# Small fp32 products of both chunks interleaved over the array, and index dots on 64 rows, in a two-layer hybrid decoder trunk

## Chip, cores and metric

The kernel runs on one core of a Trainium2 chip. The metric is the device time of one execution in microseconds (us), the median of several runs; lower is better.

## What is computed

Two decoder layers act on x of 256 tokens by 1024 features, all in float32. Each layer normalises x, makes one wide projection, feeds three token mixers (a gated DeltaNet, a pooling mixer, a sparse attention), gates and merges their outputs, and adds one output projection to x. Two places matter here.

The sparse attention picks for every query the 64 causal keys with the largest index score. There are 4 index heads of 64 features, and one index key per position that all heads share:

```
dots = einsum('bqhd,bsd->bqhs', qi, ki)             # 4 heads, 64 features
score = einsum('bqh,bqhs->bqs', wi, relu(dots))     # weighted sum over heads
score = where(causal, score, -inf);  _, idx = top_k(score, 64)
```

The DeltaNet works by chunks and needs for every chunk and head the inverse of a unit lower triangular matrix:

```
lmat = where(strict, einsum('id,jd->ij', k_beta, k) * decay, 0)
tmat = triangular_solve(eye + lmat, eye)
u = tmat @ v_beta;  w = tmat @ (k_beta * exp(gc))
```

The kernel uses two chunks of 128 tokens (the reference's chunk of 64 is a matter of association, not of result), so there are 2 chunks x 4 heads = 8 matrices of 128 x 128 a layer.

## The kernel before

**Work and staging.** Weights come from HBM in 512 KB pieces (tile raw, SyncE's queue). Each is split into an upper part wh (a cast, on ScalarE or VectorE) and a remainder wl (a subtraction on VectorE), so that a product of float32 numbers becomes three fast matmuls (wslot, lines 679 to 690). These full matmuls, 128 rows by 128 columns of the array with 256 or 512 columns streamed, write the PSUM banks called pj and are most of TensorE's work. All smaller products write the four banks called mx. Small ones are plain fp32 and leave two matmul records each in the trace.

**Index dots** (lines 865 to 903). Queries of 128 tokens are transposed into qiT[t]: two heads side by side, the first head's 64 features on rows 0 to 63, the second's on rows 64 to 127. The shared key is transposed into two tiles kiT[0] and kiT[1] (128 rows, 256 columns), zeroed at the start: kiT[0] holds the key on rows 0 to 63 and zeros below, kiT[1] the other way round (lines 670 to 672, 871 and 872). So a dot of one head is a product over all 128 rows, half of them zeros. For each of the two query blocks (t = 0 sees 128 keys, t = 1 sees 256) and each pair of heads, two dots go to one bank, ScalarE applies the ReLU, and VectorE sums with the weights wiw into score. Eight rounds of max and match_replace find the top 64.

**The triangular inverse** (lines 1154 to 1229). First VectorE inverts the four 32 x 32 diagonal blocks of all 8 matrices together in xi, 31 steps of shuffle, multiply and add (the 32-wide solve). Then the off-diagonal parts follow on TensorE in four stages, each a set of small products, a copy out of PSUM, and the next:

- p1: per chunk and head, for a = 0 and 1 (rows 0 to 31 and rows 64 to 95), 32 x 32 products, written to rows 32 to 63 and 96 to 127; copied to y1
- p2: 32 x 32 products from y1 and xi on rows 32 to 63 and 96 to 127; copied into q4 and, transposed, into tt
- p3: per chunk and head one 64 x 64 product from rows 0 to 63, written to rows 64 to 127; copied to y2
- p4: per chunk and head one 64 x 64 product from rows 64 to 127, written to rows 0 to 63; copied into q4, the finished inverse Qm[c]

The source rows of a product set which rows of the array it uses, the rows it is written to which columns. In every stage all heads of chunk 0 come first, then those of chunk 1, and both chunks use the same places.

**What sets the order.** The program only lists operations; a planner (class Plan, lines 185 to 543) simulates five engine queues and writes out an order for all of them. Each operation has a price (cost, line 221), a priority in program order for TensorE and a due time for the others; six passes are made and the one with the least planned time is kept. Copies listed for ScalarE and elementwise work listed for POOL may go to VectorE where the planner finds that better. On TensorE a change between small and full products is priced at SWITCH = 103 ns, and for REST = 2500 ns after a return to full products, full ones go first. What counts as small is the filled share of the array, rows times columns over 16384 (fill, below 0.3 before). All instructions are issued from one line (543), so the profile names that line for everything; groups are told apart by tiles and shapes.

Of the kernel before, what the change touches and what calls it, by code (L numbers as in the profile page):

```python
# [15 lines left out]
T = 256  # L16
# [168 lines left out]
class Plan:  # L185
# [35 lines left out]
    def cost(self, eng, call, args, kw):  # L221


        out = args[0]
        n = int(np.prod(out.shape[1:])) if len(out.shape) > 1 else 1
        if call == "dma_start":
            run = int(args[1].shape[-1]) * 4
            rate = 120.0 if run < 512 else 262.0 if run < 1024 else 318.0 if run < 4096 else 338.0
            return 550.0 if eng == "POOL" else 475.0, n * out.shape[0] * 4 / rate, False
        if eng == "PE":  # L230
            if call == "transpose":
                return 109.0, 170.0, False
            if args[1].ap.dtype == F32R:
                return (n / 2.4 + 13.3 if n > 100 else 60.0), 175.0, False
            m, k = args[1].shape[-1], args[1].shape[0]
            if k <= 32:
                return 21.0, 170.0, False
            if k <= 64:
                return 134.0, 170.0, False
            return 2 * (max(n, m) / 1.2 + 3), 170.0, False  # L240
        srcs = [a for a in args[1:] if isinstance(a, Ref)]
        space = [r.tile.tag.psum for r in srcs]
        ps = any(space)
        w = max([int(np.prod(r.shape[1:])) for r in srcs] + [n])
        acc = kw.get("accum_out") is not None
        if eng == "ACT":
            hold = (18 if ps else 78) + 0.875 * w
            if isinstance(kw.get("bias"), Ref) or isinstance(kw.get("scale"), Ref):
                hold += 100
            return hold + (120 if acc else 0), (95 if ps else 22) + (90 if acc else 0), False  # L250
        if eng == "POOL":
            if kw.get("op") == ALU.pow:
                return 405.0 + 151 * n, 10.0, False
            if call == "memset":
                return 50 + 0.8 * n, 50.0, False
            return 90 + 2.2 * w, 60.0, True
        if call == "reciprocal":
            return 70 + 6.0 * w, 80.0, False
        fast = call in ("tensor_copy", "tensor_scalar") and not ps and not out.tile.tag.psum
        hold = 66 + (0.52 if fast or call == "memset" else 1.045) * w  # L260
        if call in ("scalar_tensor_tensor", "tensor_scalar") and any(isinstance(a, Ref) for a in args[2:3]):
            hold += 58
        if call == "stream_shuffle":
            hold += 40
        if call == "transpose":
            hold = 464.0
        two = [r for r in ([args[1], args[2]] if call == "tensor_tensor" else
                           [args[1], args[3]] if call == "scalar_tensor_tensor" else [])]
        port = fast or (bool(two) and not any(isinstance(r, Ref) and r.tile.tag.psum for r in two))
        return hold + (65 if acc else 0), 80.0 + (30 if acc else 0), port  # L270
# [81 lines left out]
    def lay_out(self):  # L352
# [63 lines left out]
        def pick(e):  # L416

            while soon[e] and not live(soon[e][0]):
                heapq.heappop(soon[e])
            while now[e] and not live(now[e][0]):  # L420
                heapq.heappop(now[e])
            t = free[e]
            while soon[e] and soon[e][0][0] <= t:
                q = heapq.heappop(soon[e])
                if live(q):
                    heapq.heappush(now[e], q[1:])
            if not now[e]:
                while soon[e] and not live(soon[e][0]):
                    heapq.heappop(soon[e])
                if not soon[e]:  # L430
                    return None
                q = soon[e][0][1:]
                return clear(self.ops[q[1]], e, soon[e][0][0]), e, q
            if e == "PE" and not small and t < whole + REST and fill(self.ops[now[e][0][1]]) < 0.3:
                for q in heapq.nsmallest(40, now[e]):
                    if live(q) and fill(self.ops[q[1]]) > 0.9:
                        return t, e, q
            first = now[e][0]
            at = clear(self.ops[first[1]], e, t)
            if at > t:  # L440
                for q in heapq.nsmallest(12, now[e]):
                    o = self.ops[q[1]]
                    if live(q) and clear(o, e, t) <= t and held(o, e) <= at - t + SLACK:
                        return t, e, q
            return at, e, first
# [5 lines left out]
        while len(order) < len(self.ops):  # L451
# [47 lines left out]
                        z.reader, z.until = e, at + o.cost + o.tail + 36.0  # L499
            o.start = at  # L500
            if e == "PE":
                part = fill(o) < 0.3
                free[e] = clock.run(at, o.cost + (SWITCH if part != small else 0.0), fill(o))
                if small and not part:
                    whole = at
# [42 lines left out]
def trunk(ctx: ExitStack, tc: tile.TileContext, x, norm_g, w_in, gate_b, conv_w, a_log, dt_bias, dn_onorm,  # L548
# [118 lines left out]
    plan.shift = 0  # L667
    ipad = make("ipad", [128, 384])
    G.memset(ipad, 0.0)
    kiT = [make(f"kiT{i}", [128, T], F32) for i in range(2)]  # L670
    for i in range(2):
        G.memset(kiT[i], 0.0)


    def rsqrt(dst, src):
        G.tensor_tensor(dst, src, mhalf[:, :src.shape[-1]], op=ALU.pow)
# [31 lines left out]
    for l in range(DEPTH):  # L708
# [141 lines left out]
        for t in range(2):  # L850
# [18 lines left out]
            S.copy(qt, pq[:, :256])  # L869
            qiT.append(qt)  # L870
            for i in range(2):
                S.copy(kiT[i][64 * i:64 * i + 64, t * 128:(t + 1) * 128], pq[0:64, 256:384])

        wiw = make("wiw", [128, 2, 4], F32)
        V.tensor_scalar(wiw, sm[:, :, 0:4], 1.0 / 16, None, op0=ALU.mult)
# [3 lines left out]
        for t in range(2):  # L879
            n = 128 * (t + 1)  # L880
            acc = make("score", [128, 256], F32)
            for pr in range(2):
                pd = bank("mx")
                for i in range(2):
                    mm(pd[:, i * 256:i * 256 + n], qiT[t][:, pr * 128:(pr + 1) * 128], kiT[i][:, :n], True, True)
                rl = unit()
                S.activation(v2(rl)[:, :, :n], v2(pd)[:, :, :n], AF.Relu)
                for i in range(2):
                    h = pr * 2 + i
                    w = wiw[:, t, h:h + 1]  # L890
                    if h == 0:
                        V.tensor_scalar(acc[:, :n], v2(rl)[:, i, :n], w, None, op0=ALU.mult)
                    else:
                        V.scalar_tensor_tensor(acc[:, :n], v2(rl)[:, i, :n], w, acc[:, :n], op0=ALU.mult, op1=ALU.add)
            V.tensor_tensor(acc[:, n - 128:n], acc[:, n - 128:n], con("ncaus"), op=ALU.add)
            top = small(8, "top")
            for r in range(8):
# [295 lines left out]
        y1 = unit().rearrange("p (a n j) -> p a n j", a=2, n=8)  # L1193
        pairs = [(a, slice(64 * a, 64 * a + 32), slice(64 * a + 32, 64 * a + 64)) for a in range(2)]

        for c in range(2):
            c4 = slice(4 * c, 4 * c + 4)
            p1 = bank("mx")[:, :256].rearrange("p (a h j) -> p a h j", a=2, h=4)
            for h in range(4):
                for a, lo32, hi32 in pairs:  # L1200
                    mm(p1[hi32, a, h], v4(Um[c])[lo32, h, hi32], tt[lo32, 4 * c + h, 0:32], True, True)
            for a, lo32, hi32 in pairs:
                (S.copy if a else V.tensor_copy)(y1[hi32, a, c4], p1[hi32, a])
        Qm = []
        for c in range(2):
            c4 = slice(4 * c, 4 * c + 4)
            u4 = v4(Um[c])
            q = unit()
            q4 = v4(q)
            G.tensor_tensor(q.rearrange("p (h b j) -> p h b j", h=4, b=4),  # L1210
                            xi[:, c4, None, :].to_broadcast([128, 4, 4, 32]),
                            con("bd").rearrange("p (b j) -> p b j", b=4)[:, None, :, :]
                            .to_broadcast([128, 4, 4, 32]), op=ALU.mult)
            p2 = bank("mx")[:, :256].rearrange("p (a h j) -> p a h j", a=2, h=4)
            for h in range(4):
                for a, lo32, hi32 in pairs:
                    mm(p2[lo32, a, h], y1[hi32, a, 4 * c + h], xi[hi32, 4 * c + h], True, True)
            V.transpose(tt[32:64, c4, 0:32], p2[0:32, 0])
            for a, lo32, hi32 in pairs:
                S.copy(q4[lo32, :, hi32], p2[lo32, a])  # L1220
            p3 = bank("mx").rearrange("p (a h j) -> p a h j", a=2, h=4)
            for h in range(4):
                mm(p3[64:128, 0, h], u4[0:64, h, 64:128], tt[0:64, 4 * c + h], True, True)
            y2 = unit()[:, :256].rearrange("p (h j) -> p h j", h=4)
            V.tensor_copy(y2[64:128], p3[64:128, 0])
            for h in range(4):
                mm(p3[0:64, 1, h], y2[64:128, h], q4[64:128, h, 64:128], True, True)
            S.copy(q4[0:64, :, 64:128], p3[0:64, 1])
            Qm.append(q)


        yah = make("y", [128, 4, T], F32R)
# [154 lines left out]
```

## Time and profile before

| | us |
|---|---|
| median of 3 runs | 568.51 (568.05 to 568.52) |
| the profiled execution | 569.16 |
| its span, first to last instruction | 567.1 |
| TensorE busy | 560.5 |
| VectorE busy | 507.3 |
| ScalarE busy | 301.0 |
| POOL busy | 30.8 |

The engines are PE (TensorE matmuls), PEld (TensorE weight loads), DVE (VectorE), ACT (ScalarE), POOL and SP (SyncE, which issues the transfers). A group of instructions is named by what it writes and reads, as in mx<-kiT,qiT; the tile name u stands for many general work tiles. A row of the timeline gives the start, the time from the first start to the last end of a merged group, the engine, the operation with the tiles, the active rows*columns of the array, the operand's shape, and the count; in brackets stands idle time before it and what ended that. Matmuls are pipelined: a record's length is far longer than the step from one start to the next, and the step is what a matmul costs.

### The profile page before, as it was taken

The page shows a single profiled execution, that of the slowest core. Times are in us where ns is not written, and L with a number is a line of the kernel's source. Part 1 is how long each engine was busy: PE and PEld are TensorE (multiplying, and loading weights), DVE is VectorE, ACT ScalarE, POOL GpSimd, SP SyncE. Part 2 cuts the span into 40 slices and gives each one's busy share as a digit, 9 for nine tenths or more (in the row PEclk, how much of TensorE's full clock was granted, in tenths as well). Part 3 has the DMA queues.
Part 4 walks back from the last instruction along what each step waited for, and adds up shares of the span by engine and source line. Part 5 has one row for each costly group of instructions (what it writes and reads, how often), then busy time and mean ns, then how long its engine had stood idle before and what let it go on. Part 6 is the DMA issues. An engine that isn't in the chain of part 4 may idle for free. (4 is left out here: it accounts for less than half of the span.)

```text
span 567.1 us, 9577 instructions
## 1 busy us (share of the span) xinstructions
PE 560.5 (99%) x3462; PEld 495.0 (87%) x3462; DVE 507.3 (89%) x1140; ACT 301.0 (53%) x575; POOL 30.8 (5%) x45
## 2 busy tenths in 40 slices
PE   8999999999999999999999999999999999999997
PEld 7888999999888887888879889999998888888886
DVE  4999999999999999688599999999999999968672
ACT  6756556564553435554366644756484444345520
POOL 4300100001000000010010002000100000000000
PEclk9999999999999999999999999999999999999999
DMA  8884865472776666444546459457466767454512
GB/s 295 205 278 111 231 156 145 127 223 96 241 236 202 207 202 189 166 129 153 180 132 192 125 143 252 113 150 205 115 189 208 210 202 218 127 181 141 174 39 74
DMA packets 89791, 98.68 MB, mean 174 GB/s; under 512 B 5616, under 2 KB 58656, under 8 KB 89744
## 3 DMA queue, kind: packets, MB, share of 16 engines
q1 hardware_dynamic: 89184, 97.47, 58.1%
q0 software_dynamic: 560, 0.60, 0.6%
q8 instruction: 27, 0.44, 0.3%
q14 instruction: 20, 0.16, 0.1%
HBM read 97.01 MB, written 1.05 MB: 173 GB/s over the span
## 5 line engine op out<-in xcount | busy, mean ns | idle before, releaser
L543 ACT CAST wh<-raw 128x1024 fp32r<-128x1024 f32 (+1 forms) x168 | 175.6, 1050 | 137.9 <-PE pj L543 107.4
L543 DVE TENSOR_TENSOR wl<-raw,wh 128x1024 fp32r<-128x1024 f32 (+1 forms) x174 | 209.3, 1212 | 10.6 <-issue 2.9
L543 PE MATMUL pj<-wh,hl 128*128 128x512 f32 (+1 forms) x352 | 101.5, 388 | 0.5 <-DVE hl L543 0.5
L543 PE MATMUL pj<-wl,hh 128*128 128x512 f32 (+1 forms) x352 | 101.4, 388 | 0.0
L543 PE MATMUL pj<-wh,hh 128*128 128x512 f32 (+1 forms) x352 | 100.6, 387 | 0.5 <-ACT hh L543 0.5
L543 PEld LDWEIGHTS pj<-wh,hl 128*128 128x128 f32 x352 | 64.9, 188 | 13.9 <-DVE hl L543 2.0
L543 PEld LDWEIGHTS pj<-wh,hh 128*128 128x128 f32 x352 | 64.7, 188 | 12.8 <-ACT hh L543 1.1
L543 PEld LDWEIGHTS pj<-wl,hh 128*128 128x128 f32 x352 | 64.8, 188 | 11.8
L543 PE MATMUL pj<-hh,wl 128*128 128x256 f32 x384 | 55.3, 284 | 0.0
L543 PE MATMUL pj<-hh,wh 128*128 128x256 f32 x384 | 55.1, 285 | 0.0
L543 PE MATMUL pj<-hl,wh 128*128 128x256 f32 x384 | 54.4, 283 | 0.0
L543 PE MATMUL pj<-wh,y 128*128 128x512 f32 (+1 forms) x208 | 50.5, 381 | 0.0
L543 PEld LDWEIGHTS pj<-hh,wh 128*128 128x128 f32 x384 | 49.8, 192 | 0.2
L543 PEld LDWEIGHTS pj<-hh,wl 128*128 128x128 f32 x384 | 50.0, 192 | 0.0
L543 PEld LDWEIGHTS pj<-hl,wh 128*128 128x128 f32 x384 | 49.6, 192 | 0.0
L543 PEld LDWEIGHTS pj<-wh,y 128*128 128x128 f32 x208 | 38.7, 188 | 7.6
L543 PE MATMUL mx<-wh,y 128*128 128x512 f32 (+1 forms) x128 | 38.4, 380 | 0.0
L543 PEld LDWEIGHTS mx<-u,u 128*128 128x128 f32 (+2 forms) x336 | 30.9, 165 | 3.8 <-issue 1.8
L543 PE MATMUL mx<-u,u 128*128 128x128 f32 (+2 forms) x336 | 32.5, 249 | 0.6 <-DVE u L543 0.5
L543 DVE SCALAR_TENSOR_TENSOR u<-pj,pt,u 128x255 f32<-128x255 f32 (+2 forms) x72 | 29.6, 474 | 0.2 <-ACT u L543 0.2
L543 PE MATMUL pj<-wl,y 128*128 128x512 f32 (+1 forms) x104 | 28.4, 382 | 0.0
L543 PEld LDWEIGHTS mx<-wh,y 128*128 128x128 f32 x128 | 23.3, 188 | 4.4 <-DVE y L543 0.2
(204 smaller groups left out, 677.4 us busy)
## 6 DMA issues: line engine op xcount, KB each, us to landing
raw<-in_w_in_dram SPq DMA_DIRECT2D x128, 512.0 KB, 4.2
raw<-in_w_branch_dram SPq DMA_DIRECT2D x24, 512.0 KB, 3.8
raw<-in_w_out_dram SPq DMA_DIRECT2D x16, 512.0 KB, 3.5
tg<-in_gate_b_dram SPq DMA_DIRECT2D x12, 256.0 KB, 4.3
raw<-in_w_in_dram SPq DMA_DIRECT2D x4, 486.0 KB, 5.4
x_sb<-in_x_dram SPq DMA_DIRECT2D x2, 512.0 KB, 4.5
out_dram<-x_sb SPq DMA_DIRECT2D x3, 256.0 KB, 2.0
raw<-in_w_in_dram SPq DMA_DIRECT2D x2, 324.0 KB, 4.2
```

What stands on the lines that cost most here:

```text
L543: getattr(self.real[o.eng], o.call)(*[put(a) for a in o.args], **{k: put(v) for k, v in o.kw.items()})
```

## The change

- The two zero-padded key tiles become one tile with the key on rows 0 to 63 and again on rows 64 to 127; the memsets go.
- A dot takes only the 64 rows of its head. Heads on rows 0 to 63 and heads on rows 64 to 127 alternate; heads of one half share a bank, so that each ReLU covers heads h and h + 2.
- In p1 to p4 the head loop is outside and the chunk loop inside, so products of chunk 0 and chunk 1 alternate, and chunk 1 is written to other rows (in p1 and p2 the 32 rows beside those of chunk 0, in p3 and p4 the other half), that is, uses other columns of the array. Each stage is done for both chunks before the next is listed.
- The planner's prices for small products change, and its bound for a small product rises from 0.3 to 0.6 of the array, which takes in the dots (64 x 128, 0.5).

```diff
--- before.py
+++ after.py
@@ -234,9 +234,9 @@
                 return (n / 2.4 + 13.3 if n > 100 else 60.0), 175.0, False
             m, k = args[1].shape[-1], args[1].shape[0]
             if k <= 32:
-                return 21.0, 170.0, False
+                return 16.0, 170.0, False
             if k <= 64:
-                return 134.0, 170.0, False
+                return 58.0 * max(n / 64.0, 1.0), 170.0, False
             return 2 * (max(n, m) / 1.2 + 3), 170.0, False
         srcs = [a for a in args[1:] if isinstance(a, Ref)]
         space = [r.tile.tag.psum for r in srcs]
@@ -431,7 +431,7 @@
                     return None
                 q = soon[e][0][1:]
                 return clear(self.ops[q[1]], e, soon[e][0][0]), e, q
-            if e == "PE" and not small and t < whole + REST and fill(self.ops[now[e][0][1]]) < 0.3:
+            if e == "PE" and not small and t < whole + REST and fill(self.ops[now[e][0][1]]) < 0.6:
                 for q in heapq.nsmallest(40, now[e]):
                     if live(q) and fill(self.ops[q[1]]) > 0.9:
                         return t, e, q
@@ -499,7 +499,7 @@
                         z.reader, z.until = e, at + o.cost + o.tail + 36.0
             o.start = at
             if e == "PE":
-                part = fill(o) < 0.3
+                part = fill(o) < 0.6
                 free[e] = clock.run(at, o.cost + (SWITCH if part != small else 0.0), fill(o))
                 if small and not part:
                     whole = at
@@ -667,10 +667,7 @@
     plan.shift = 0
     ipad = make("ipad", [128, 384])
     G.memset(ipad, 0.0)
-    kiT = [make(f"kiT{i}", [128, T], F32) for i in range(2)]
-    for i in range(2):
-        G.memset(kiT[i], 0.0)
-
+    kiT = make("kiT", [128, T], F32)
 
     def rsqrt(dst, src):
         G.tensor_tensor(dst, src, mhalf[:, :src.shape[-1]], op=ALU.pow)
@@ -869,7 +866,7 @@
             S.copy(qt, pq[:, :256])
             qiT.append(qt)
             for i in range(2):
-                S.copy(kiT[i][64 * i:64 * i + 64, t * 128:(t + 1) * 128], pq[0:64, 256:384])
+                S.copy(kiT[64 * i:64 * i + 64, t * 128:(t + 1) * 128], pq[0:64, 256:384])
 
         wiw = make("wiw", [128, 2, 4], F32)
         V.tensor_scalar(wiw, sm[:, :, 0:4], 1.0 / 16, None, op0=ALU.mult)
@@ -879,19 +876,21 @@
         for t in range(2):
             n = 128 * (t + 1)
             acc = make("score", [128, 256], F32)
+
+            pd = [bank("mx") for _ in range(2)]
             for pr in range(2):
-                pd = bank("mx")
                 for i in range(2):
-                    mm(pd[:, i * 256:i * 256 + n], qiT[t][:, pr * 128:(pr + 1) * 128], kiT[i][:, :n], True, True)
-                rl = unit()
-                S.activation(v2(rl)[:, :, :n], v2(pd)[:, :, :n], AF.Relu)
-                for i in range(2):
-                    h = pr * 2 + i
-                    w = wiw[:, t, h:h + 1]
-                    if h == 0:
-                        V.tensor_scalar(acc[:, :n], v2(rl)[:, i, :n], w, None, op0=ALU.mult)
-                    else:
-                        V.scalar_tensor_tensor(acc[:, :n], v2(rl)[:, i, :n], w, acc[:, :n], op0=ALU.mult, op1=ALU.add)
+                    mm(v2(pd[i])[:, pr, :n], qiT[t][64 * i:64 * i + 64, pr * 128:(pr + 1) * 128],
+                       kiT[64 * i:64 * i + 64, :n], True, True)
+            rl = [unit() for _ in range(2)]
+            for i in range(2):
+                S.activation(v2(rl[i])[:, :, :n], v2(pd[i])[:, :, :n], AF.Relu)
+            for h in range(4):
+                w, r = wiw[:, t, h:h + 1], v2(rl[h % 2])[:, h // 2, :n]
+                if h == 0:
+                    V.tensor_scalar(acc[:, :n], r, w, None, op0=ALU.mult)
+                else:
+                    V.scalar_tensor_tensor(acc[:, :n], r, w, acc[:, :n], op0=ALU.mult, op1=ALU.add)
             V.tensor_tensor(acc[:, n - 128:n], acc[:, n - 128:n], con("ncaus"), op=ALU.add)
             top = small(8, "top")
             for r in range(8):
@@ -1193,40 +1192,44 @@
         y1 = unit().rearrange("p (a n j) -> p a n j", a=2, n=8)
         pairs = [(a, slice(64 * a, 64 * a + 32), slice(64 * a + 32, 64 * a + 64)) for a in range(2)]
 
+
+        c4s = [slice(4 * c, 4 * c + 4) for c in range(2)]
+        b1, b2 = ([bank("mx")[:, :256].rearrange("p (a h j) -> p a h j", a=2, h=4) for _ in range(2)]
+                  for _ in range(2))
+        for h in range(4):
+            for c in range(2):
+                for a, lo32, hi32 in pairs:
+                    mm(b1[c][(hi32, lo32)[c], a, h], v4(Um[c])[lo32, h, hi32], tt[lo32, 4 * c + h, 0:32], True, True)
         for c in range(2):
-            c4 = slice(4 * c, 4 * c + 4)
-            p1 = bank("mx")[:, :256].rearrange("p (a h j) -> p a h j", a=2, h=4)
-            for h in range(4):
-                for a, lo32, hi32 in pairs:
-                    mm(p1[hi32, a, h], v4(Um[c])[lo32, h, hi32], tt[lo32, 4 * c + h, 0:32], True, True)
             for a, lo32, hi32 in pairs:
-                (S.copy if a else V.tensor_copy)(y1[hi32, a, c4], p1[hi32, a])
-        Qm = []
+                (S.copy if a else V.tensor_copy)(y1[hi32, a, c4s[c]], b1[c][(hi32, lo32)[c], a])
+        Qm = [unit() for _ in range(2)]
         for c in range(2):
-            c4 = slice(4 * c, 4 * c + 4)
-            u4 = v4(Um[c])
-            q = unit()
-            q4 = v4(q)
-            G.tensor_tensor(q.rearrange("p (h b j) -> p h b j", h=4, b=4),
-                            xi[:, c4, None, :].to_broadcast([128, 4, 4, 32]),
+            G.tensor_tensor(Qm[c].rearrange("p (h b j) -> p h b j", h=4, b=4),
+                            xi[:, c4s[c], None, :].to_broadcast([128, 4, 4, 32]),
                             con("bd").rearrange("p (b j) -> p b j", b=4)[:, None, :, :]
                             .to_broadcast([128, 4, 4, 32]), op=ALU.mult)
-            p2 = bank("mx")[:, :256].rearrange("p (a h j) -> p a h j", a=2, h=4)
-            for h in range(4):
+        for h in range(4):
+            for c in range(2):
                 for a, lo32, hi32 in pairs:
-                    mm(p2[lo32, a, h], y1[hi32, a, 4 * c + h], xi[hi32, 4 * c + h], True, True)
-            V.transpose(tt[32:64, c4, 0:32], p2[0:32, 0])
+                    mm(b2[c][(lo32, hi32)[c], a, h], y1[hi32, a, 4 * c + h], xi[hi32, 4 * c + h], True, True)
+        for c in range(2):
+            V.transpose(tt[32:64, c4s[c], 0:32], b2[c][(pairs[0][1], pairs[0][2])[c], 0])
             for a, lo32, hi32 in pairs:
-                S.copy(q4[lo32, :, hi32], p2[lo32, a])
-            p3 = bank("mx").rearrange("p (a h j) -> p a h j", a=2, h=4)
-            for h in range(4):
-                mm(p3[64:128, 0, h], u4[0:64, h, 64:128], tt[0:64, 4 * c + h], True, True)
-            y2 = unit()[:, :256].rearrange("p (h j) -> p h j", h=4)
-            V.tensor_copy(y2[64:128], p3[64:128, 0])
-            for h in range(4):
-                mm(p3[0:64, 1, h], y2[64:128, h], q4[64:128, h, 64:128], True, True)
-            S.copy(q4[0:64, :, 64:128], p3[0:64, 1])
-            Qm.append(q)
+                S.copy(v4(Qm[c])[lo32, :, hi32], b2[c][(lo32, hi32)[c], a])
+        half = slice(0, 64), slice(64, 128)
+        b3 = [bank("mx").rearrange("p (a h j) -> p a h j", a=2, h=4) for _ in range(2)]
+        for h in range(4):
+            for c in range(2):
+                mm(b3[c][half[1 - c], 0, h], v4(Um[c])[0:64, h, 64:128], tt[0:64, 4 * c + h], True, True)
+        y2 = [unit()[:, :256].rearrange("p (h j) -> p h j", h=4) for _ in range(2)]
+        for c in range(2):
+            (S.copy if c else V.tensor_copy)(y2[c][64:128], b3[c][half[1 - c], 0])
+        for h in range(4):
+            for c in range(2):
+                mm(b3[c][half[c], 1, h], y2[c][64:128, h], v4(Qm[c])[64:128, h, 64:128], True, True)
+        for c in range(2):
+            S.copy(v4(Qm[c])[0:64, :, 64:128], b3[c][half[c], 1])
 
 
         yah = make("y", [128, 4, T], F32R)
```

## Rows read from the trace of the kernel before

**Rows 1.** The page, busy time of each engine, and the granted clock in 40 slices.
```profile
PE 560.5 (99%) x3462; PEld 495.0 (87%) x3462; DVE 507.3 (89%) x1140; ACT 301.0 (53%) x575; POOL 30.8 (5%) x45
...
PEclk9999999999999999999999999999999999999999
```

**Rows 2.** Waits of TensorE, longest and last line; first and last long piece of the chain.
```profile
PE mx L543 <- POOL wh L543: 1.1, 1, 1.1
...
PE pj L543 <- DVE hl L543: 0.5, 1, 0.5
...
363.10 1.56 PE mx L543 x14
...
562.50 1.45 PE pj L543 x12
```

**Rows 3.** Stretches: us, busy PE, PEld, DVE, ACT, POOL, clock, DMA share, GB/s.
```profile
60.00:90.00 30.00, 29.67 (x251) 29.49 (x250) 30.00 (x70) 17.35 (x33) 2.02 (x2) 1.00 0.77 203
...
150.00:180.00 30.00, 30.00 (x134) 24.85 (x133) 28.85 (x93) 13.85 (x16) 0.00 (x0) 1.00 0.68 205
...
210.00:240.00 30.00, 29.48 (x229) 24.37 (x229) 23.76 (x47) 15.04 (x29) 1.29 (x1) 1.00 0.56 183
...
480.00:510.00 30.00, 30.00 (x235) 25.04 (x234) 24.32 (x48) 12.55 (x25) 0.94 (x1) 1.00 0.53 163
```

**Rows 4.** Timeline of TensorE where the first 32-row products start, both layers.
```profile
221.15 0.69 PE L543 MATMUL mx<-u,u 32*32 32x32 f32 x32 [0.52 <-DVE u L543]
...
489.99 0.69 PE L543 MATMUL mx<-u,u 32*32 32x32 f32 x32
```

**Rows 5.** Matmuls by shape: count | busy us, mean ns of one | idle before.
```profile
L543 PE MATMUL mx<-u,u 64*64 64x64 f32 x64 | 4.6, 221 | 0.0
...
L543 PE MATMUL mx<-kiT,qiT 128*128 128x256 f32 x16 | 3.8, 379 | 0.0
...
L543 PE MATMUL mx<-kiT,qiT 128*128 128x128 f32 x16 | 2.1, 277 | 0.0
...
L543 PE MATMUL mx<-xi,u 32*32 32x32 f32 x64 | 1.4, 192 | 0.0
```

**Rows 6.** Timeline around the index dots of layer 0.
```profile
34.51 1.10 PE L543 MATMUL mx<-kiT,qiT 128*128 128x128 f32 x8
...
37.16 1.89 PE L543 MATMUL mx<-kiT,qiT 128*128 128x256 f32 x8
...
39.34 0.63 PE L543 MATMUL pj<-wh,hh 128*128 128x512 f32 x2
...
39.60 0.28 DVE L543 TENSOR_SCALAR score<-u,wiw 128x128 f32<-128x128 f32 x1
```

**Rows 7.** Timeline of TensorE around a run of 32-row products, layer 0.
```profile
223.75 0.86 PE L543 MATMUL pj<-wh,hl 128*128 128x512 f32 x3
...
224.54 0.69 PE L543 MATMUL mx<-xi,u 32*32 32x32 f32 x32
...
225.16 0.51 PE L543 MATMUL pj<-wh,hl 128*128 128x512 f32 x1
...
225.51 1.08 PE L543 MATMUL pj<-wl,hh 128*128 128x512 f32 x4
```

**Rows 8.** Timeline around a run of 64-row products, layer 0.
```profile
227.88 1.00 PEld L543 LDWEIGHTS mx<-u,u 64*64 64x64 f32 x16 [0.35 <-issue]
227.88 1.14 PE L543 MATMUL mx<-u,u 64*64 64x64 f32 x16
...
229.52 1.09 PE L543 MATMUL pj<-wl,hh 128*128 128x512 f32 x4
...
229.76 1.05 ACT L543 CAST wh<-raw 128x1024 fp32r<-128x1024 f32 x1 [1.71 <-issue]
...
230.45 1.07 PE L543 MATMUL pj<-wh,hh 128*128 128x512 f32 x4
```

**Rows 9.** Timeline of TensorE, 227.80 to 228.00 us: records running there.
```profile
227.88 0.32 PE L543 MATMUL mx<-u,u 64*64 64x64 f32 x2
```


## The prediction

> **What bounds the kernel now.** I read the page first. TensorE's row says 99% of the span, VectorE's 89%, and the granted clock is at full in every slice [rows 1]. A busy share of 99% can hide waits, since matmuls are pipelined, so the waits and the chain come next. TensorE has five lines of waits, from 1.1 us in all (at the start) down to 0.5 each, and the chain of waits is TensorE work without a break from 363.10 us to its last piece at 562.50 [rows 2]. So TensorE is the bound: time taken off it is time off the span, as long as the others keep up. The table by stretch shows where that is doubtful. VectorE is as good as full from 30 to 210 us (six stretches, 28.85 to 30.00 of each 30), and has over 5 us of air in each 30 where the small products run (210 to 240 and 480 to 510) [rows 3]. What VectorE does in the full stretch ends in the 32-wide solve. Just then, at 221.15, TensorE waits 0.52 us for it; in the second layer, at 489.99, it doesn't [rows 4].
>
> All instructions share one helper line, so I go by shapes. An fp32 product leaves two matmul records. The index dots are 16 records of 128 columns and 16 of 256, the 32-row products 64 records in p1 and 64 more in p2, the 64-row products 64 [rows 5]. The whole change lies in these.
>
> **The change, part by part.**
>
> *Index dots, their pace.* Today every dot takes all 128 rows, half of them zeros. In layer 0 the short run is 8 records over 1.10 us, the last 0.275 long: (1.10 - 0.275)/7 = 0.118 us a record, 0.94 for 8. The long run is (1.89 - 0.38)/7 = 0.216 a record, 1.73 for 8 [rows 5, 6]. Both layers: 5.3 us. On 64 rows a record streams as many columns, so I count it the same when alone; the gain is that the heads on rows 0 to 63 and 64 to 127 may run side by side. No row shows 64-row, 128-column products doing so. Bounds: pace unchanged (0), or two at a time (-2.65 us). The nearest row is the run of 32-row products, which today alternates rows 0 to 31 with 64 to 95: 32 records, (0.69 - 0.19)/31 = 0.016 us a step [rows 7]. The 64-row run stays on one place of the array and steps by (1.14 - 0.22)/15 = 0.061 [rows 8]. Half the columns alone would make 0.031; the alternation gives 0.016. So two row groups do overlap, and I take -2.65.
>
> *Index dots, the way in and out.* A small product between full ones costs extra. Between 223.75 and 225.51 lie four full matmuls and one 32-row run: 1.76 us, less 4 x 0.23 (full ones step by 0.93/4, four of them from 229.52 to 230.45), less 32 x 0.016 = 0.51, leaves 0.33 [rows 7, 8]. Full-row dots pay none of it on leaving today: the last of the long run starts at 37.16 + 1.51 = 38.67 and streams for 0.216, to 38.89; two full matmuls later, 0.45, the next starts, at 39.34 [rows 6]. Half-row dots will pay, if using part of the array is what costs: 4 runs x 0.33 = +1.3 (bounds 0 and 1.3; I take 1.3, from the only small run whose surroundings I sum). The dots net -1.3 us, -0.65 a layer.
>
> *64-row products.* Four runs of 16 records at 0.061 are 3.9 us [rows 5, 8]. Now chunk 0 and chunk 1 alternate on the two column halves, over the same 64 rows. Bounds: 0, or half, -1.95. Only the 32-row run shows neighbours overlapping, and they differ in rows and columns at once, so nothing isolates columns; it is still the nearest, and I take half. In the 64-row run the weight loads (16 in 1.00 us) lie beside the matmuls (16 in 1.14, the same start) on the same rows [rows 8]. The Trainium skill, "TensorE: Matmul & The Clock Gate", Part 3, The mechanism, says that a weight load overlaps a running matmul only where the row group differs. By that rule this term would be 0 and the sum -1.65; the trace disagrees as far as one place of the array goes.
>
> *32-row products.* Four runs of 32 records, 0.51 each, 2.05 us [rows 5, 7]. They alternate two row groups already; the second chunk now comes between, on other columns. Bounds 0 and -1.0; by the same step I take -1.0. Their entering and leaving stays, 8 times.
>
> *What costs nothing.* Copies, transposes and VectorE's score sums keep number and shape. The copy of y2 for chunk 1 now prefers ScalarE, which sits idle for 1.71 us there [rows 8]. A ReLU now waits for all four dots, not two; VectorE first sums scores at 39.60, over 4 us after the first run of dots ended and 0.7 after the second [rows 6]. Without that cover the scores would come up to one run of dots, under 1 us, later into a full VectorE. The two memsets that fall away are the idlest engine's, POOL's (5% busy), at the start [rows 1]; it has nothing urgent behind them. No DMA is added or moved.
>
> *The order.* The kernel's planner gets new prices for these products and treats dots as small ones, so every queue is laid out anew and a dot can be held back up to 2.5 us behind full matmuls. Nothing in the trace prices that; I bound it by the waits it already has [rows 2]: one of 0.5 us gone, or as much again as its five lines hold, some 3 us. One part I can place: the 0.65 us that the first layer's dots save lies ahead of the full VectorE stretch, and at 221.15 TensorE already waits for VectorE [rows 3, 4]. I count it as lost there.
>
> *Sum.* -1.3 - 1.95 - 1.0 + 0.65 = -3.6 us. The profiled execution took 569.16 us (span 567.1 and 2.1 around it): it would come to 565.6. It stands 0.65 above the median of 568.51, against which the sum gives **564.9 us**.
>
> **Rivals.**
>
> *Columns alone bring nothing.* If products on the same rows take turns whatever their columns, the last two gains go: -0.65 to -1.3, 567.2 to 567.9 us. For it: no row shows two column places at once. Against: the 32-row step of 0.016, which two row groups share without a hint of a common limit.
>
> *The new order gives it back.* TensorE arrives earlier at the solve, and between the four small stages it needs full matmuls whose weights VectorE has split. If the wait at 221.15 grows by what was saved upstream, one like it opens at 489.99 and a half-microsecond opens before each of two or three stages, 2 to 3 us return: 567 to 568.5. For it: VectorE full. Against: its air where the small products stand, and a second layer with no wait there.
>
> *Slower: weight loads come out from behind the matmuls.* With each record on another place than the last, over rows in use, the load could have to wait for the matmul before. The first step of a run, where no matmul hides the load, shows that price: two 64-row records cover 0.32 us, the second 0.22 long, so 0.10 instead of 0.061 [rows 9]. At 0.04 on 64 records that is +2.6; with the dots' 0.65 and no gain on the 32-row runs it makes 568.5 + 1.9 = 570.4 us. It ends slower once the 64-row step exceeds 0.061 + (0.65 + 1.14)/64 = 0.089. The Trainium skill's rule above, taken strictly, would do this. Against: the loads lie beside matmuls on one place today.
>
> **How the numbers follow.** A measurement tells about 0.2%, 1.14 us, from no change: faster is below 567.4, slower above 569.6. The forecast has 0.52; its own range, from full gain with a lucky order to 2 us of loss, is 562.6 to 566.5. Columns bring nothing: 0.20, half faster, half same. The order gives it back: 0.16, split 0.06 faster, 0.08 same, 0.02 slower. Loads exposed: 0.12, slower. So 0.68 faster, 0.18 same, 0.14 slower. The range, 562.6 to 569.3, takes in the second and nearly all of the third case, and leaves out the last.
>
> **What would show it.** Right: dots in runs with a mean step near 0.108 (256 columns) and 0.058 (128); 64-row runs of 16 records within 0.7 us instead of 1.14, 32-row runs within 0.45 instead of 0.69; about 0.3 us of entering and leaving around each run of dots; TensorE still 99% busy and the chain on it to the end. Wrong: a 64-row step at or above 0.06, a dot step still at 0.216, or waits of TensorE for VectorE that sum to over 3 us more.

## The result, and the profile after

| | before | changed |
|---|---|---|
| median, 6 runs each, us | 568.34 (568.05 to 568.76) | 563.87 (563.61 to 564.15) |
| profiled execution, us | 569.16 | 563.87 |
| its span, us | 567.1 | 561.8 |

The ratio is 0.9919, 95% interval 0.9909 to 0.9929: 4.5 us or 0.8% faster. The forecast was 3.6 us less.

The page of the changed kernel, to be held against [rows 1]:

```profile
span 561.8 us, 9576 instructions
...
PE 555.9 (99%) x3462; PEld 489.3 (87%) x3462; DVE 508.2 (90%) x1142; ACT 300.3 (53%) x574; POOL 28.3 (5%) x42
```

TensorE is still the bound, at 99%, with the same number of matmul records; VectorE and ScalarE are as busy as before to 1 us. So as much is done as before, and TensorE is done with it sooner. Its waits, against [rows 2]:

```profile
PE mx L543 <- POOL wh L543: 1.1, 1, 1.1
PE mx L543 <- DVE big L543: 0.7, 2, 0.5
PE pj L543 <- DVE hl L543: 0.5, 1, 0.5
PE pj L543 <- ACT hh L543: 0.4, 1, 0.4
```

The line for VectorE's u, the 0.5 us ahead of the first 32-row products in layer 0, is gone. The timeline of TensorE shows that place and the runs of the first layer's inverse, against [rows 4, 7, 8]:

```profile
220.42 0.61 PE L543 MATMUL pj<-wh,hh 128*128 128x512 f32 x2
220.97 0.45 PE L543 MATMUL mx<-u,u 32*32 32x32 f32 x32
...
223.75 0.39 PE L543 MATMUL pj<-wh,hh 128*128 128x512 f32 x1
224.07 0.45 PE L543 MATMUL mx<-xi,u 32*32 32x32 f32 x32
224.45 0.96 PE L543 MATMUL pj<-wh,hh 128*128 128x512 f32 x3
225.25 1.08 PE L543 MATMUL pj<-wh,hl 128*128 128x512 f32 x4
226.17 1.07 PE L543 MATMUL pj<-wl,hh 128*128 128x512 f32 x4
227.17 0.68 PE L543 MATMUL mx<-u,u 64*64 64x64 f32 x16
227.78 1.19 PE L543 MATMUL pj<-wh,hh 128*128 128x512 f32 x4
228.81 1.08 PE L543 MATMUL pj<-wh,hl 128*128 128x512 f32 x4
```

A 32-row run takes 0.45 us instead of 0.69, a 64-row run 0.68 instead of 1.14. In steps: (0.45 - 0.19)/31 = 0.008 us instead of 0.016, and (0.68 - 0.22)/15 = 0.031 instead of 0.061. What such a run costs the stream of full matmuls: from 223.75 to 225.25 are 1.50 us with four full ones of 0.23 in them, leaves 0.58 where it was 0.84; from 226.17 to 228.81 are 2.64 with eight, leaves 0.80 where it was 1.26. The 1.26 is read the same way before: from 227.34 to the 229.52 of [rows 8] are 2.18 us with four full ones in them.

```profile
227.34 0.61 PE L543 MATMUL pj<-wh,hl 128*128 128x512 f32 x2
...
228.95 0.73 PE L543 MATMUL pj<-wh,hl 128*128 128x512 f32 x2
```

The weight loads of the same 64-row run, and its first 80 ns (a window that ends at 227.25):

```profile
227.17 0.54 PEld L543 LDWEIGHTS mx<-u,u 64*64 64x64 f32 x16 [0.35 <-issue]
```

```profile
227.17 0.27 PE L543 MATMUL mx<-u,u 64*64 64x64 f32 x2
```

The 16 loads, too, take half of the 1.00 us that they took [rows 8]. Two matmuls begin before 227.25 and together cover 0.27 us, the length of the first record of a run (its later ones are 0.22 long): they start practically at once, on the same rows and different columns.

The long run of dots in layer 0, against [rows 6], and the short one in layer 1:

```profile
37.37 0.61 PE L543 MATMUL pj<-wh,hh 128*128 128x512 f32 x2
37.92 1.13 PE L543 MATMUL mx<-kiT,qiT 64*128 64x256 f32 x8
38.98 0.73 PE L543 MATMUL pj<-wh,hl 128*128 128x512 f32 x2
39.55 0.62 PE L543 MATMUL pj<-wl,hh 128*128 128x512 f32 x2
...
306.20 0.39 PE L543 MATMUL pj<-wh,hh 128*128 128x512 f32 x1
306.52 0.71 PE L543 MATMUL mx<-kiT,qiT 64*128 64x128 f32 x8
307.17 0.50 PE L543 MATMUL pj<-wh,hh 128*128 128x512 f32 x1
307.50 0.63 PE L543 MATMUL pj<-wh,hl 128*128 128x512 f32 x2
```

The short one of layer 1 before:

```profile
309.08 0.39 PE L543 MATMUL pj<-wh,hh 128*128 128x512 f32 x1
309.31 1.05 PE L543 MATMUL mx<-kiT,qiT 128*128 128x128 f32 x8
310.12 0.48 PE L543 MATMUL pj<-wh,hh 128*128 128x512 f32 x1
310.43 0.63 PE L543 MATMUL pj<-wh,hl 128*128 128x512 f32 x2
```

The long one costs 2.18 - 4 x 0.23 = 1.26 us instead of 1.73; the short one 1.30 - 2 x 0.23 = 0.84 instead of 1.35 - 2 x 0.23 = 0.89. The two-at-a-time pace is there, and so is a price for entering and leaving that dots on all rows did not pay.

### The profile page after: what moved, and what is told of

Read it like the earlier page. It is cut to its first block, busy times and chain, and to the rows that moved or that the text cites. A ratio compares the mean times of both kernels' runs of the same rounds, so it can differ in the third digit from the quotient of the medians.

```text
span 561.8 us, 9576 instructions
## 1 busy us (share of the span) xinstructions
PE 555.9 (99%) x3462; PEld 489.3 (87%) x3462; DVE 508.2 (90%) x1142; ACT 300.3 (53%) x574; POOL 28.3 (5%) x42
## 3 DMA queue, kind: packets, MB, share of 16 engines
HBM read 97.01 MB, written 1.05 MB: 175 GB/s over the span
## 4 chain that ended last, share of the span: by engine, by line
PE 94%; DVE 4%; DMA 1%; issue 0%; SPq 0%; ACT 0%; DVEq 0%
PE pj L543 76%; PE mx L543 18%; DVE wl L543 2%; DMA raw<-in_w_in_dram 1%; DVE score L543 1%; DVE top L543 1%; SPq L543 0%; DVE big L543 0%; DVE u L543 0%; ACT wh L543 0%; DVE z L543 0%; DVE mxm L543 0%; DVE x_sb L543 0%; DVE hl L543 0%; DVE bad L543 0%
## 5 line engine op out<-in xcount | busy, mean ns | idle before, releaser
L543 PE MATMUL pj<-wh,hl 128*128 128x512 f32 (+1 forms) x352 | 99.9, 387 | 0.5 <-DVE hl L543 0.5
L543 PEld LDWEIGHTS mx<-u,u 128*128 128x128 f32 (+2 forms) x336 | 28.6, 164 | 3.0 <-issue 1.4
L543 PE MATMUL mx<-u,u 128*128 128x128 f32 (+2 forms) x336 | 30.1, 250 | 0.0
```

The source lines that it names most:

```text
L543: getattr(self.real[o.eng], o.call)(*[put(a) for a in o.args], **{k: put(v) for k, v in o.kw.items()})
```

## Experiments

My theory was that the time comes from the shorter steps, less what entering and leaving costs. The rival to be kept apart from it was the order: new prices make the planner lay out every queue anew. Ratios below are to the kernel before, measured beside each run. All kernels below have the new prices and the new bound, unless it is said otherwise.

### Each half of the change alone

Dots as changed, the inverse's products as before:

```diff
-for h in range(4):
-    for c in range(2):
-        for a, lo32, hi32 in pairs:
-            mm(b1[c][(hi32, lo32)[c], a, h], ...)
+for c in range(2):
+    for h in range(4):
+        for a, lo32, hi32 in pairs:
+            mm(p1[hi32, a, h], ...)
...
```

> The index dots as in the changed kernel, the small products of the inverse as before. My theory (the gain is the shorter step of the runs, less the entering and leaving of each new small run): dot steps 0.063 and 0.108 us, 64-row runs back at a step of 0.061, 32-row runs at 0.016; time 0.8 to 1.3 us below the kernel before, ratio 0.9977 to 0.9986. Rival (the new order of all queues is where the time comes from): any ratio from 0.993 to 1.003, with the steps as said. A third theory, that entering and leaving eats all of the dots' gain: ratio 1.000.

Measured: 566.71 us, ratio 0.9965 (0.9953 to 0.9978), 1.9 us less than before. The steps are mostly as expected (0.108 in the long runs, 0.016 and 0.061 in those of the inverse, 0.063 in the short run of layer 1; the short run of layer 0 steps by 0.081). The time is not: 1.9 us is above the 0.8 to 1.3 of my theory and more than the dots' own 2 x (0.47 + about 0.05) = 1.0 us. The timeline shows where some of the rest lies:

```profile
220.01 0.61 PE L543 MATMUL pj<-wh,hh 128*128 128x512 f32 x2
220.56 0.69 PE L543 MATMUL mx<-u,u 32*32 32x32 f32 x32
```

The wait ahead of the first 32-row run is not there. TensorE's waits in the profiled execution come to 1.5 us in all, where they were 3.4 before. The other half, the inverse's products as changed and the dots on all rows:

```diff
-mm(v2(pd[i])[:, pr, :n], qiT[t][64 * i:64 * i + 64, pr * 128:(pr + 1) * 128], kiT[64 * i:64 * i + 64, :n], True, True)
+mm(pd[:, i * 256:i * 256 + n], qiT[t][:, pr * 128:(pr + 1) * 128], kiT[i][:, :n], True, True)
```

> The products of the inverse as in the changed kernel, index dots on all 128 rows as before. My theory: 64-row steps 0.031, 32-row steps 0.0085, dot steps 0.216; four 64-row runs give 4 x 0.46 and four 32-row runs 4 x 0.25, together -2.8 us, ratio 0.995, and 0.994 if the wait of 0.5 us ahead of the first 32-row run goes with them. Rival (order): anywhere from 0.992 to 1.002, not the sum of the steps.

Measured: 566.36 us, ratio 0.9959 (0.9947 to 0.9972), 2.3 us less. The steps are the expected ones, and here the wait stays:

```profile
219.00 1.07 PE L543 MATMUL pj<-wh,hl 128*128 128x512 f32 x4
220.62 0.45 PE L543 MATMUL mx<-u,u 32*32 32x32 f32 x32 [0.55 <-DVE u L543]
```

So the products save 2.8 us by their steps, of which 2.3 arrive; where the rest stays was not found. The two halves together, 4.2 us, are the change's 4.5 within the intervals.

### The prices alone

No product is changed; the planner gets the new prices and the new bound:

```diff
-                return 21.0, 170.0, False
+                return 16.0, 170.0, False
...
-                return 134.0, 170.0, False
+                return 58.0 * max(n / 64.0, 1.0), 170.0, False
...
-                part = fill(o) < 0.3
+                part = fill(o) < 0.6
```

> The kernel before with the planner's new prices and its new bound for a small product, no product changed. My theory: the steps stay as before (0.216, 0.061, 0.016) and the time stays within 0.6 us, ratio 0.999 to 1.001. Rival (order): at least 0.6 us of the 4.5 gained shows here, ratio below 0.999, with the wait ahead of the first 32-row run gone.

Measured: 568.44 us, ratio 0.9997 (0.9988 to 1.0006), no difference. The wait is still there, 0.44 us. The opposite, the changed products with the old prices and bound:

> The changed kernel's products with the planner's old prices and its old bound for a small product. My theory (steps on the array give the time, the prices little): same steps as in the changed kernel, 563.5 to 564.5 us, ratio 0.991 to 0.993. Rival (the prices and the new bound for small ones give the order without the wait ahead of the first 32-row run): that wait of some 0.5 us is back, 564.5 to 566 us, ratio 0.993 to 0.996.

Measured: a median of 564.11 us, ratio 0.9935 (0.9914 to 0.9956), which the changed kernel's own ratio beside it (0.9915, below) lies within. The median hides a spread: four of the six executions took 563.6 to 564.4 us, two took 566.1 and 567.3. The trace, of the fastest, has the steps of the changed kernel, except in the short run of layer 0, and 0.2 us of the wait for VectorE's u. The prices by themselves give nothing that can be measured here.

The changed kernel once more, measured beside these:

> The changed kernel once more, beside the others of this job. Every theory: 563.9 us, ratio 0.992. It stands here so that the others can be set against it on the same chip.

Measured: 563.87 us, ratio 0.9915 (0.9902 to 0.9928).

### The same columns for both chunks

The chunks still alternate, in separate banks, but write the same rows:

```diff
-mm(b1[c][(hi32, lo32)[c], a, h], v4(Um[c])[lo32, h, hi32], tt[lo32, 4 * c + h, 0:32], True, True)
+mm(b1[c][hi32, a, h], v4(Um[c])[lo32, h, hi32], tt[lo32, 4 * c + h, 0:32], True, True)
...
-mm(b3[c][half[1 - c], 0, h], v4(Um[c])[0:64, h, 64:128], tt[0:64, 4 * c + h], True, True)
+mm(b3[c][half[1], 0, h], v4(Um[c])[0:64, h, 64:128], tt[0:64, 4 * c + h], True, True)
...
```

> The changed kernel, but both chunks' products write the same rows and so use the same columns, as before; they still alternate, and still write different banks. My theory (different columns of the array run side by side): 64-row steps back at 0.058 to 0.061, 32-row steps at 0.016, time 2.8 us above the changed kernel, ratio to the kernel before 0.997. Rival (alternating chunks and banks is enough, the place does not matter): steps stay at 0.031 and 0.0085, ratio 0.992.

Measured: 566.39 us, ratio 0.9961 (0.9948 to 0.9975), about the time of the dots alone. The runs in its timeline are those of the kernel before:

```profile
223.47 0.69 PE L543 MATMUL mx<-xi,u 32*32 32x32 f32 x32
...
226.81 1.14 PE L543 MATMUL mx<-u,u 64*64 64x64 f32 x16
```

So alternating chunks and banks brings nothing; different columns do it all. The order cannot be behind it: in the two traces TensorE, VectorE, ScalarE and POOL run the same operations on the same tiles in the same order as in the changed kernel. This is the run that isolates columns, which the trace of before could not.

### Dots in blocks, and dots on one half

The loops over halves and pairs are exchanged, so that the queue holds both products of the upper half, then both of the lower:

```diff
-            for pr in range(2):
-                for i in range(2):
+            for i in range(2):
+                for pr in range(2):
```

> The changed kernel with the dots listed by half: both products on rows 0 to 63, then both on rows 64 to 127, instead of in turn. My theory (two halves run side by side only where neighbours in the queue lie on different rows): within a half the step is 0.216 for 256 columns, at most the one neighbouring pair overlaps, so a long run covers 1.3 to 1.8 us from first to last start instead of 0.76 and a short one 0.65 to 0.8 instead of 0.44; two layers lose 1.5 to 2.5 us, ratio to the kernel before 0.995 to 0.997. Rival (a product on 64 rows is itself twice as fast as one on 128): steps stay at 0.108 and 0.063, ratio 0.992.

Measured: 564.54 us, ratio 0.9927 (0.9915 to 0.9938). My expectation missed: the run is as short as with alternation.

```profile
37.96 1.14 PE L543 MATMUL mx<-kiT,qiT 64*128 64x256 f32 x8
39.03 0.73 PE L543 MATMUL pj<-wh,hl 128*128 128x512 f32 x2
```

The first 40 ns of that run (a window that ends at 38.00) already hold two records:

```profile
37.96 0.49 PE L543 MATMUL mx<-kiT,qiT 64*128 64x256 f32 x2
```

The rival, that a product on 64 rows is itself twice as fast, would explain it, but ScalarE speaks against it. It sat idle until the first half's bank was full, and that was at 39.13, at the end of the whole run and not in its middle:

```profile
39.13 0.60 ACT L543 ACTIVATE u<-mx 128x512 f32<-128x512 f32 x1 [2.66 <-PE mx L543]
```

So I formed another theory, that each half works through its own products whatever their order, and put it to the test by giving all dots to one half:

```diff
-mm(v2(pd[i])[:, pr, :n], qiT[t][64 * i:64 * i + 64, pr * 128:(pr + 1) * 128], kiT[64 * i:64 * i + 64, :n], True, True)
+mm(v2(pd[i])[:, pr, :n], qiT[t][0:64, pr * 128:(pr + 1) * 128], kiT[0:64, :n], True, True)
```

> The changed kernel, but all dots take rows 0 to 63: heads 0 and 2 are computed twice, heads 1 and 3 are left out, everything else is the same work. It asks why the dots listed in blocks kept the pace of the alternating ones. My theory now (each half of the array works through its own products, whatever their order in the queue): with one half in use the step is 0.216 for 256 columns and 0.108 for 128, the runs cover 1.5 and 0.8 us, two layers lose 2 to 2.6 us, time 565.9 to 566.5, ratio 0.996. Rival (a product on 64 rows takes half the time of one on 128, alone as well): steps 0.108 and 0.063, 563.9 us, ratio 0.992.

Measured: 565.70 us, ratio 0.9951 (0.9938 to 0.9965). By the ratios that is 1.8 us above the changed kernel, a little less than the 2 to 2.6 expected. 
```profile
38.03 1.99 PE L543 MATMUL mx<-kiT,qiT 64*128 64x256 f32 x8
39.95 0.73 PE L543 MATMUL pj<-wh,hl 128*128 128x512 f32 x2
```

A window that ends at 38.20, 0.17 us into the run, holds only one record of it:

```profile
38.03 0.48 PE L543 MATMUL mx<-kiT,qiT 64*128 64x256 f32 x1
```

(1.99 - 0.38)/7 = 0.230 us a record: a product on half the rows takes as long as one on all (0.216), plus the entering, which is in the first step. The gain is the two halves side by side and nothing else. So in the kernel with dots in blocks the second record that began at once must have been one of the lower half, which stands behind all of the upper half in the queue. That kernel has the steps of the changed one and took 0.7 us more than it did beside it; the intervals overlap, so this is no more than a hint of what the order of the queues does.

### One run of dots a layer

If entering and leaving costs 0.3 us a run, two runs fewer should pay. The transposes of both query blocks share two banks and are copied together; all eight dots then come at once:

```diff
...
-            qt = make("qiT", [128, 256], F32)
-            S.copy(qt, pq[:, :256])
-            qiT.append(qt)
-            for i in range(2):
-                S.copy(kiT[64 * i:64 * i + 64, t * 128:(t + 1) * 128], pq[0:64, 256:384])
+        qt = make("qiT", [128, 512], F32)
+        S.copy(qt, pq2)
+        qiT = [qt[:, t * 256:(t + 1) * 256] for t in range(2)]
+        for i in range(2):
+            S.copy(kiT[64 * i:64 * i + 64, :], pk2[0:64, :256])
...
+        for t in (1, 0):
+            n = 128 * (t + 1)
+            for pr in range(2):
+                for i in range(2):
+                    mm(v2(pds[t][i])[:, pr, :n], ...)
...
```

> The changed kernel with the dots of both query blocks in one run a layer: the transposes of both blocks share two banks and are copied together, so that all eight dots are ready at once. My theory: each run costs some 0.33 us to enter and leave, so two runs fewer give 0.6 to 0.7 us against the changed kernel, less what the later scores cost: 563.1 to 563.6, ratio 0.990 to 0.991. Rival (the scores, 2 to 3 us later into a full VectorE, and the four banks held at once cost more): 564 to 566 us, ratio 0.992 to 0.996, with a wait of TensorE on VectorE around 220 us again.

Measured: 562.82 us, ratio 0.9895 (0.9883 to 0.9908), the fastest kernel here; its four runs (562.69 to 562.96) lie below all runs of the changed kernel beside it (563.52 to 564.54). But the reason is not the one I gave. Layer 1:

```profile
310.29 0.40 PE L543 MATMUL pj<-wh,hl 128*128 128x512 f32 x1
310.62 1.77 PE L543 MATMUL mx<-kiT,qiT 64*128 64x256 f32 x16
312.31 0.50 PE L543 MATMUL pj<-wh,hl 128*128 128x512 f32 x1
312.65 0.62 PE L543 MATMUL pj<-wl,hh 128*128 128x512 f32 x2
```

The merged run costs 2.36 - 2 x 0.23 = 1.90 us, the two runs of the changed kernel 1.26 + 0.84 = 2.10: 0.2 us, not 0.33. In layer 0 the same sum gives 2.17, no gain. So of the 1.05 us at most a fifth is the merged run; the rest came with the new order and copies, and what in them brought it was not tried. TensorE's waits, 2.0 us here and 2.4 in the changed kernel beside it, are no proof: in its two profiled executions the changed kernel itself has 2.7 and 2.4.

## Why the prediction was right

- **The bound.** TensorE was the bound and stayed it; what its runs lost in time the span lost.
- **64-row products.** Forecast -1.95 us, measured 4 x (1.26 - 0.80) = -1.8. Half was the right end of the bounds, but it was a choice: no row of before told 0 from half, and only the run with the same columns does. The loads of such a run, all on the same rows, took 0.54 us instead of 1.00 and lie beside their matmuls. The Trainium skill, "TensorE: Matmul & The Clock Gate", Part 3, The mechanism, has a weight load overlap a running matmul only where the row group differs; the same section also lets a load run ahead into a background weight buffer. Taken strictly, the first of the two does not hold here, and the measurement decides.
- **32-row products.** Forecast -1.0, measured 4 x (0.84 - 0.58) = -1.0, again a choice between bounds that came out.
- **Dots.** Forecast -2.65 by the pace and +1.3 by entering and leaving, -1.3 net; measured -0.47 in a long run and -0.05 in a short one, -1.0 net. The pace was right; entering and leaving is mis-sized, about 0.4 us a run (1.26 less 8 x 0.108 = 0.86) where the 32-row run had given 0.33.
- **The step that failed** is the +0.65 under *The order*: the first layer's saving was to be lost in a longer wait at 221.15. That wait of 0.5 us went instead. VectorE, which was to hold TensorE up there, began the two transposes that the run waits for 0.57 us earlier (the lines below, before and changed). And TensorE had more to do until then: 1338 of its records stand ahead of the run instead of 1332, six full matmuls or 1.4 us more. The dots alone have 1338 ahead and no wait; the two kernels with full-row dots and the new prices have 1332 ahead and waits of 0.55 and 0.44 us; half-row dots with the old prices have 1331 and 0.2 us. So in the changed kernel full matmuls that the planner lists earlier stand where the wait was. Why it lists them so stays open, and they are not the only way: with the dots on one half there are 1332 ahead and no wait either.

```profile
220.67 0.89 DVE L543 STREAM_TRANSPOSE u<-xi 128x256 f32<-128x256 f32 x2
...
220.10 0.90 DVE L543 STREAM_TRANSPOSE u<-xi 128x256 f32<-128x256 f32 x2
```

- **The sum, and luck in it.** With -3.9 us from the runs and -0.5 from the wait the sum is -4.4, against 4.5 measured. The two errors had opposite signs, 0.4 too much from the runs and 1.15 too little from the order, which brought the forecast nearer. Nor is -4.4 a full account: between the two profiled executions the span fell by 5.3 us. That of before lay 0.8 us above its median (569.16 against 568.34), and what made it so was not found.
- **Rivals.** That columns bring nothing is refuted by the run with the same columns, from the other side: with them the steps of the inverse's products are the old ones again and about 2.5 of its 2.8 us are lost. Exposed weight loads would have shown as a 64-row step above 0.089; it was 0.031. That the order gives it back did not happen. That a new order can move a kernel by 0.5 to 1 us is suggested by the single run of dots (1.05 us, of which the merged run is at most a fifth) and was not shown by itself.

## What to carry to other kernels

Small products on a bound TensorE are priced by the columns that they stream and by the places of the array that they share, not by how many rows they fill: give independent ones different rows or different columns, and in these fp32 runs they went side by side. Count 0.3 to 0.4 us for each stretch of them among full matmuls, as here, where it ate 1.6 of the 2.6 us that the dots' pace saved. Where a planner lays out all queues anew, up to about a microsecond may be its share, and only runs that change one part at a time tell it from the part's own; best is one that leaves the order as it is, like the run with the same columns.

## What the runs showed of the hardware

- Order in the queue did not matter for two halves of rows, which I had not expected: four products listed as upper, upper, lower, lower ran as two pairs, 1.14 us against 1.13 for the alternating list. A product of the lower half began while those listed ahead of it still ran or had not begun.
- Products on the two column halves over the same 64 rows overlap fully: 0.031 us a step against 0.061, weight loads included (16 in 0.54 us against 1.00). 32-row products on four places instead of two step by 0.008 instead of 0.016.
- A product on 64 of 128 rows is not faster by itself: 0.230 us a record against 0.216 on all rows, and the difference is the first step of the run.
